# An encoder trunk in fp32: HGRN output as plain products, last value panels as block products, a root on PSUM

## The chip, the cores and the metric

The kernel runs on one core of a Trainium2 chip. The metric is the device time of one execution in microseconds (us). Five engines work side by side: TensorE (PE, matmuls into PSUM banks; PEld is its weight load), VectorE (DVE), ScalarE (ACT), GpSimd (POOL), and SyncE (SP), which issues the DMAs. Each engine executes its own list of instructions in order and waits on semaphores for the others.

## The reference

The trunk has four sub-layers with residuals on a sequence of T = 1024 tokens and D = 1024 channels: a gMLP mixer, a gated ConvFFN, an HGRN2 mixer and a second ConvFFN. Each begins with an RMSNorm whose shift, scale and gate come from a conditioning vector (adaLN, 96 rows of modulation in blocks of 128, each a dot product of a 128x1024 weight block with the vector).

```python
# gMLP:  z = gelu(h @ w_in); u, v = split(z); v = layernorm(v)
s = jnp.einsum('hnm,bcmhd->bcnhd', ws, v) + b_s.T[None, None, :, :, None]
return (u * s.reshape(bsz, t, GM_WIDTH)) @ w_out
# HGRN2: q, fz, i, g = split(h @ w_in, 4); o = gated linear scan over 8 heads
o = o * lax.rsqrt(jnp.mean(o * o, axis=-1, keepdims=True) + EPS)
o = (o.reshape(bsz, t, HG_HEADS * HG_VAL) * gn_g.astype(jnp.float32)).astype(h.dtype)
return (o * jax.nn.silu(g)) @ w_out
# ConvFFN: y = causal conv of width 3 over h @ w_up; (gelu(gate) * val) @ w_down
```

All inputs, parameters and the output are fp32.

## The kernel before

The activations stay in SBUF as `xT`: channels on partitions, 8 tiles of 128 channels, 1024 tokens in two halves of 512 (LO and HI). Matrix products run as three products of split operands, hi·hi, hi·lo and lo·hi (`mm3`, L273). `p_split` makes the parts: ScalarE writes the rounded hi (L471), DVE or GpSimd subtracts it from the source to get lo (L474).

Most products are block products: a pair of 2×2 blocks is multiplied with 7 products instead of 8. That needs sums of operand blocks (`p_comb`, L481, also inside `combos` and `sums`) and additions of results. `Pairs` does it for the up products (`GmUp` for the gMLP, `HgUp` for HGRN, `Ffn`), and `block_out` for the output and down products.

The stages in order, with their places in the profiled execution:

- values, 19 to 252 us: the gMLP's v, 32 tiles of 128 tokens by 512 channels in 4 panels; the first half of the tokens of panels 0 and 1 goes along with the first norm. The rest follows behind the second half's norm. Panels 2 and 3 use plain products (`v_tile`). Beside them DVE works off modulation dots (`ada_dot`, L281), 512 KB loaded for each.
- `GmUp`, 252 to 393: u in 8 pairs, of which the first two are plain (`nplain`), with the spatial product and the gate multiply (L1258). The normalised x is made once more for the block sums: `entry` loads x again and DVE re-normalises it (L1276). Gated blocks and their sums go to DRAM (`gact`).
- `block_out` of the gMLP, 393 to 564, with the next norm (L334 statistics, ten DVE instructions L307 to L317 as inverse root, L339, L344 broadcast, L348 copy) behind its halves; first FFN up (to 985) and down (to 1206).
- HGRN, 1206 to 1683: 16 scan units (8 heads × 2 halves). A unit's output passes a transpose (L1654) and a multiply with the gate (L1656), and goes to DRAM as `hact`, 7 blocks per two heads, sums made on the way.
- HGRN output, to 1833: `block_out` over 4 pairs of heads, each evacuation adding to `xT` on DVE (L413, `p_evac`). Second FFN up and down, final norm.

The order of the instructions of each engine is not written by hand. A `Plan` takes each operation with engine, estimated cost, reads, writes and a priority, schedules the lists against one another twice (the second time by how late an operation may be for PE's list), and emits the lists. A changed cost or priority so moves instructions on all engines.

## Time and profile before

| what | value |
|---|---|
| time, median of 3 runs (lowest to highest) | 2420.84 us (2420.24 to 2420.99) |
| profiled execution, its own time | 2421.06 us |
| its span, first to last instruction | 2419.3 us |
| mean granted TensorE clock | 0.993 |
| DVE, ACT, POOL busy | 2062.3, 1280.9, 458.5 us |
| DMA | 340.34 MB, mean 141 GB/s |

A row of the groups gives line, engine, operation, output<-inputs, tile shape and count, then busy time and mean nanoseconds of one, then the idle time ahead of the group on its engine and who ended it. In a timeline a row is a run of equal instructions with its start, its duration and, in brackets, the wait before it. In the windows an engine's busy time in a stretch stands beside the number of its instructions, then PE's granted clock, the DMA share and the rate.

### The profile page before, as it was taken

The page shows a single profiled execution, that of the slowest core. Times are in us where ns is not written, and L with a number is a line of the kernel's source. Part 1 is how long each engine was busy: PE and PEld are TensorE (multiplying, and loading weights), DVE is VectorE, ACT ScalarE, POOL GpSimd, SP SyncE. Part 2 cuts the span into 40 slices and gives each one's busy share as a digit, 9 for nine tenths or more (in the row PEclk, how much of TensorE's full clock was granted, in tenths as well). Part 3 has the DMA queues.
Part 4 walks back from the last instruction along what each step waited for, and adds up shares of the span by engine and source line. Part 5 has one row for each costly group of instructions (what it writes and reads, how often), then busy time and mean ns, then how long its engine had stood idle before and what let it go on. Part 6 is the DMA issues. An engine that isn't in the chain of part 4 may idle for free.

```text
span 2419.3 us, 32969 instructions
## 1 busy us (share of the span) xinstructions
PE 2381.5 (98%) x11382; PEld 1983.2 (82%) x11382; DVE 2062.3 (85%) x3331; ACT 1280.9 (53%) x2274; POOL 458.5 (19%) x303
## 2 busy tenths in 40 slices
PE   9999999999999999999999999999999999999998
PEld 7888787888888888888788888888777888888887
DVE  8888997898998898976798777879899988989756
ACT  4424664455555455445566666666455554554544
POOL 0122110222222222013201111111322222220121
PEclk9999999999999999999999999999999999999999
DMA  9797678721333333844201111215403333338332
GB/s 354 274 347 274 222 239 299 263 82 35 101 118 114 105 104 116 293 131 140 82 19 49 57 47 54 70 58 182 132 18 105 113 114 105 105 118 291 96 103 98
DMA packets 160873, 340.34 MB, mean 141 GB/s; under 512 B 16193, under 2 KB 35009, under 8 KB 160706
## 3 DMA queue, kind: packets, MB, share of 16 engines
q1 hardware_dynamic: 160706, 338.25, 42.3%
q8 instruction: 89, 1.46, 0.2%
q14 instruction: 78, 0.64, 0.1%
HBM read 259.01 MB, written 79.17 MB: 140 GB/s over the span
## 4 chain that ended last, share of the span: by engine, by line
PE 89%; DVE 5%; DMA 2%; issue 2%; ACT 1%; POOL 0%; SPq 0%; POOLq 0%; DVEq 0%; ACTq 0%
PE pb L273 82%; PE pb L1546 4%; PE pb L1242 1%; DVE n L474 1%; PE pb L1611 1%; DMA raw<-in_ada 1%; PE pb L1631 1%; DVE raw L876 1%; DVE w L474 1%; DVE h L474 0%; PE pb L1633 0%; DMA h<-act 0%; DVE w L481 0%; DVE h L281 0%; PE pb L1453 0%
## 5 line engine op out<-in xcount | busy, mean ns | idle before, releaser
L273 PE MATMUL pb<-h,w 128*128 128x512 f32 (+1 forms) x4338 | 1011.7, 389 | 5.3 <-ACT h L471 2.9
L273 PEld LDWEIGHTS pb<-h,w 128*128 128x128 f32 x4338 | 809.0, 188 | 177.6 <-ACT h L471 4.2
L273 PE MATMUL pb<-n,w 128*128 128x512 f32 x3312 | 791.7, 392 | 6.6 <-DVE n L474 2.5
L273 PEld LDWEIGHTS pb<-n,w 128*128 128x128 f32 x3312 | 617.2, 188 | 138.5 <-DVE n L474 4.1
L474 POOL TENSOR_TENSOR w<-w,w 128x512 fp32r<-128x512 f32 x158 | 248.6, 1579 | 888.5 <-ACT w L471 771.6
L471 ACT ACTIVATE w<-w 128x512 fp32r<-128x512 f32 x384 | 237.0, 627 | 236.1 <-PE pb L273 135.5
L876 DVE SCALAR_TENSOR_TENSOR raw<-wk,prm,raw 128x1024 f32<-128x1024 f32 x168 | 267.8, 1604 | 6.0 <-ACT raw L872 5.0
L474 DVE TENSOR_TENSOR w<-w,w 128x512 fp32r<-128x512 f32 x226 | 162.9, 726 | 35.8 <-ACT w L471 34.9
L273 PE MATMUL pb<-w,n 128*128 128x512 f32 x768 | 177.8, 393 | 4.2 <-DVE n L459 3.6
L471 ACT ACTIVATE w<-n 128x512 fp32r<-128x512 f32 x136 | 85.9, 631 | 168.8 <-PE pb L273 158.2
L273 PEld LDWEIGHTS pb<-w,n 128*128 128x128 f32 x768 | 145.1, 189 | 36.0 <-DVE n L459 4.0
L711 ACT ACTIVATE wk<-pb 128x512 f32<-128x512 f32 x160 | 94.4, 593 | 134.1 <-PE pb L273 111.8
L474 DVE TENSOR_TENSOR w<-n,w 128x512 fp32r<-128x512 f32 x136 | 99.0, 730 | 65.7 <-ACT w L471 65.1
L714 DVE TENSOR_TENSOR wk<-pb,wk 128x512 f32<-128x512 f32 x160 | 108.3, 686 | 44.9 <-PE pb L273 40.6
L474 POOL TENSOR_TENSOR w<-raw,w 128x512 fp32r<-128x512 f32 (+1 forms) x52 | 84.6, 1636 | 275.6 <-ACT w L471 204.3
L471 ACT ACTIVATE h<-h 128x512 fp32r<-128x512 f32 x198 | 121.7, 617 | 16.1 <-DMA h<-act 5.3
L872 ACT ACTIVATE raw<-wk,prm 128x1024 f32<-128x1024 f32 x84 | 103.6, 1240 | 31.7 <-DVE raw L481 15.1
L474 DVE TENSOR_TENSOR h<-h,h 128x512 fp32r<-128x512 f32 x150 | 108.0, 723 | 4.8 <-ACT h L471 4.8
L474 POOL TENSOR_TENSOR h<-h,h 128x512 fp32r<-128x512 f32 x48 | 69.6, 1449 | 215.8 <-ACT h L471 208.9
L413 DVE SCALAR_TENSOR_TENSOR xT<-pb,mod,xT 128x512 f32<-128x512 f32 (+1 forms) x120 | 83.0, 729 | 25.1 <-PE pb L273 24.7
L281 DVE SCALAR_TENSOR_TENSOR h<-h,raw 128x1024 f32<-128x1024 f32 x81 | 102.6, 1293 | 1.0 <-DMA h<-in_ada 0.9
L1556 ACT ACTIVATE wk<-wk 128x256 f32<-128x256 f32 x192 | 75.1, 417 | 42.9 <-PE pb L1546 33.6
(261 smaller groups left out, 2969.5 us busy)
## 6 DMA issues: line engine op xcount, KB each, us to landing
w<-in_up SPq DMA_DIRECT2D x88, 512.0 KB, 3.7
h<-in_ada SPq DMA_DIRECT2D x81, 512.0 KB, 6.0
act<-raw SPq DMA_DIRECT2D x154, 256.0 KB, 2.2
h<-act SPq DMA_DIRECT2D x124, 256.0 KB, 2.7
n<-in_down SPq DMA_DIRECT2D x64, 256.0 KB, 5.3
h<-gact SPq DMA_DIRECT2D x56, 256.0 KB, 3.5
gact<-xT SPq DMA_DIRECT2D x52, 256.0 KB, 3.7
vd<-h SPq DMA_DIRECT2D x32, 256.0 KB, 4.1
```

The costliest lines, as they stand in the source:

```text
L273: PE.matmul(ps, L[i // 2], R[i % 2], start=first and i == 0 and not more, stop=last and i == 2, skip_group_check=more)
L281: V.scalar_tensor_tensor(out=raw, in0=raw, scalar=1.0, in1=condr, op0=ALU.mult, op1=ALU.mult, accum_out=mod[:, m:m + 1])
L413: V.scalar_tensor_tensor(out=xT[:, d, hs], in0=ps.f, scalar=gate(d), in1=xT[:, d, hs], op0=ALU.mult, op1=ALU.add)
L471: pl.op("S", 0.2 + 0.43 * w, lambda: S.activation(hi.r, src.f, AF.Copy), r=(src,), w=(hi,), pr=pr)
L474: lambda: e.tensor_tensor(out=lo.r, in0=src.f, in1=hi.f, op=ALU.subtract), *preds,
L711: pl.op("S", 0.6, lambda: S.activation(c.f, ps.f, func), r=(ps,), w=(c,), pr=p(i) - 10)
L714: pl.op("V", 0.69, lambda: V.tensor_tensor(out=c.f, in0=ps.f, in1=c.f, op=ALU.add), r=(ps, c), w=(c,), pr=p(i) - 8)
L872: pl.op("S", 1.22, lambda: S.activation(y.f, wk[:, o + PADW:o + PADW + T], AF.Identity, bias=pc("conv_b", l * NUP + b), scale=cw(2)), r=(c ...
L876: pl.op("V", 1.26, lambda w=w: V.scalar_tensor_tensor(out=y.f, in0=wk[:, o + w:o + w + T], scalar=cw(w), in1=y.f, op0=ALU.mult, op1=ALU.ad ...
L1242: PE.matmul(ps.f[:, i * P:(i + 1) * P], v.f[:, i * P:(i + 1) * P], wsT[:, j, :], start=True, stop=True)
L1546: PE.matmul(ps_()[0:m, c, :], K.f[:, c * P:c * P + m], q, start=True, stop=True)
L1556: S.activation(halves_(X2, s)[:, :, i, :], halves_(X, s)[:, :, i, :], AF.Copy)
```

## The change

Five parts.

1. The HGRN output becomes plain: for each head and each block of 128 output channels one `mm3` into a bank that sums over 8 heads. A head's output is stored as it is (two blocks per head, the last two heads stay in SBUF) and split on the way back. Weights come in 8 loads of 512 KB instead of 16 of 256 KB.
2. Value panels 2 and 3 of the values become block products, as do pairs 0 and 1 of `GmUp`; both share the block sums of the normalised x, which stays in `xT` instead of being made again (`entry` is gone).
3. In the values the inverse root of the second half's norm takes its intermediate values from PSUM (`psum_ops`, 13 instructions, cost 2.5 instead of 1.95 in the plan).
4. GpSimd's splits in the values go by 128x512 instead of 128x1024 (`half_split`).
5. The modulation dots are spread: 27 instead of 61 in the values, 7 instead of 6 in `GmUp`, 24 instead of 13 in the gMLP's output product, 22 instead of none in the first down product, for which the conditioning row passes through DRAM (`crow`). The plan counts their loads as 1.5 us later (`ADA_LAG`).

```diff
+ADA_LAG = 1.5
+NV_ADA = (18, 3)
+NU_ADA = 1
+NO_ADA = 24
+VS_ENG = "VVGGG"
...
-        return self.LOAD if eng == "D" else self.LAT if e2 != eng else self.CHAIN if eng == "V" else 0.0
+        return self.LOAD + self.late.get(i, 0) if eng == "D" else self.LAT if e2 != eng else self.CHAIN if eng == "V" else 0.0
...
-    hacts = dram.tile([NH // 2, 7, P, HT], F32, name="hact")
+    crow = dram.tile([1, D], F32, name="cr")
+    hacts = dram.tile([NH - 2, 2, P, HT], F32, name="hact")
...
+    def psum_ops(ps, n, scale):
+        m, r, q, u = (small[:, i * 4:i * 4 + n] for i in range(4))
...
+            lambda: V.tensor_copy(m, mp),
+            lambda: V.tensor_scalar(out=rp.bitcast(I32), in0=mp.bitcast(I32), scalar1=-0.5,
+                                    scalar2=float(0x5F3759DF - 2 ** 30 - 2 ** 22), op0=mul, op1=add),
+            lambda: V.tensor_copy(r, rp),
+            lambda: V.tensor_tensor(out=tp, in0=rp, in1=r, op=mul),
...
-            p_load(pl, x, a["ada"][l, blk], pr)
-            p_dot(m, x, pr + 2)
+            pl.late[p_load(pl, x, a["ada"][l, blk], pr)] = ADA_LAG
+            p_dot(m, x, pr + 2, cond=cond)
...
+        p_stats(pl, nm1, accv, bv(7), rbv[1], VB, inps=True)
...
+        def half_split(x, ws, eng, pr):
+            for o in (0, HT):
+                p_split(pl, sub(x, o, HT), *(sub(w, o, HT) for w in ws), eng, pr)
...
+        for i, (n, bn, g, more) in enumerate((("S2", "T2", 0, True), ("S1", "T1", 1, False), ("S3", "T3", 0, True),
+                                              ("A22", "T4", 0, True), ("S4", "B22", 1, True))):
...
+            for c in range(2):
+                ws = ring.next()
+                half_split(raws[n][c], ws, VS_ENG[i], pr - 4 + 2 * c)
+                for t in range(4):
+                    mms(ws, up.b[bn], c, t, 4 * g + t, c == 0, c == 1, more, pr + 2 * c + 0.5 * t)
...
-            self.acts, self.nplain = (gacts, "gact"), 2
+            self.acts = gacts, "gact"
...
-        def entry(self, k, pr):
...
+    p_ada(Seq(whole(nc_[0], F32), whole(nc_[2], F32)), len(ada_todo), DB, cond=cond)
...
-            if u % 4 == 1:
-                p_comb(pl, gout[0, 0], go, gout[0, 0], ALU.subtract, pr)
-                self.store(m, 3, gout[0, 0], pr)
...
+            if h < NH - 2:
+                pl.op("D", 0.73, lambda: nc.sync.dma_start(hacts[h, hf], go.f), r=(go,), w=(("hact", u, u + 1),), pr=pr)
...
-    block_out(pl, OB, NH // 2, lambda m, k, o: a["ho"][2 * m + k, :, o:o + HT],
...
+    def ho_mm(h, hf, d, first, final, b, pr):
+        (wh, wl), (th, tl) = (wtop if d < 4 else wlow)[h], hact[hf][h]
+        c, ps = slice(d % 4 * P, (d % 4 + 1) * P), bv(b)
+        pl.op("PE", 0.681, lambda: mm3(ps.f, (wh.r[:, c], wl.r[:, c]), (th.r, tl.r), first, final), r=(wh, wl, th, tl),
+              w=(ps,), pr=pr)
...
+    for h in range(NH):
+        for d in range(4):
+            ho_mm(h, 0, d, h == 0, h == NH - 1, 4 + d, OB + h + 0.25 * d)
```

In the changed kernel the line numbers move: `mm3` is at L280, `p_evac` at L442, the sums of squares at L459, the splits at L500 and L503, block sums at L510, the output transpose at L1749 and its multiply at L1751.

First place: DVE's list behind the inverse root of the last scan unit, where the HGRN output runs. Before (n, w and raw are operand buffers, `xT` the residual and the scan's working space):

```order
L317 SCALAR_TENSOR_TENSOR small<-small 128x4
L474 TENSOR_TENSOR n_12588<-n_12835,n_12546 128x512
L474 TENSOR_TENSOR n_12591<-w_12367,n_12455 128x512
L474 TENSOR_TENSOR n_12607<-n_12840,n_12573 128x512
L474 TENSOR_TENSOR n_12664<-w_12367,n_12579 128x512
L481 TENSOR_TENSOR n_12898<-n_12686,n_12669 128x512
L1656 SCALAR_TENSOR_TENSOR xT<-pb_77,prm,w_12418 128x512
L413 SCALAR_TENSOR_TENSOR xT<-pb_76,mod,xT 128x512
L481 TENSOR_TENSOR raw_67<-xT 128x512
L474 TENSOR_TENSOR n_12684<-n_12898,n_12593 128x512
L474 TENSOR_TENSOR n_12699<-w_12378,n_12596 128x512
```

The same place now (h_12906 is the sum of squares of the next norm):

```order
L324 SCALAR_TENSOR_TENSOR small<-small 128x4
L503 TENSOR_TENSOR h_12888<-w_12410,h_12888 128x512
L442 SCALAR_TENSOR_TENSOR xT<-pb_79,mod,xT 128x512
L442 SCALAR_TENSOR_TENSOR xT<-pb_80,mod,xT 128x512
L442 SCALAR_TENSOR_TENSOR xT<-pb_81,mod,xT 128x512
L1751 SCALAR_TENSOR_TENSOR xT<-pb_77,prm,w_12424 128x512
L442 SCALAR_TENSOR_TENSOR xT<-pb_82,mod,xT 128x512
L442 SCALAR_TENSOR_TENSOR xT<-pb_75,mod,xT 128x512
L503 TENSOR_TENSOR w_12925<-xT,w_12925 128x512
L459 TENSOR_TENSOR h_12906<-h_12906,raw_66 128x512
L442 SCALAR_TENSOR_TENSOR xT<-pb_76,mod,xT 128x512
L459 TENSOR_TENSOR h_12906<-h_12906,raw_66 128x512
```

Ahead of the unit's output multiply (L1656, now L1751) stood four splits and a block sum of the output product; now stand a split and evacuations, and behind it one split of the unit's own output. The other splits of the product are ahead of the unit's root, within the scan.

Second place: GpSimd's list in the values, from its first split on. Before:

```order
L474 TENSOR_TENSOR w_205<-raw_65,w_176 128x1024
L474 TENSOR_TENSOR w_200<-raw_66,w_166 128x1024
L474 TENSOR_TENSOR w_232<-raw_65,w_198 128x1024
L474 TENSOR_TENSOR w_275<-raw_66,w_225 128x1024
L474 TENSOR_TENSOR w_317<-raw_65,w_243 128x1024
L474 TENSOR_TENSOR w_357<-raw_66,w_273 128x1024
```

Now:

```order
L503 TENSOR_TENSOR w_622<-raw_66,w_611 128x512 x2
L503 TENSOR_TENSOR w_665<-raw_65,w_651 128x512 x2
L503 TENSOR_TENSOR w_767<-raw_65,w_736 128x512 x2
L503 TENSOR_TENSOR w_791<-raw_66,w_761 128x512 x2
L503 TENSOR_TENSOR w_861<-raw_65,w_837 128x512 x2
L503 TENSOR_TENSOR w_938<-raw_66,w_910 128x512 x2
```

Each row of 128x1024 is two of 128x512 in its place, each with a wait of its own; from the seventh on (not shown) the new rows read block sums (w) and no longer the loaded panel alone.

More of the change, by code (lines that the diff above doesn't have):

```diff
@@ L117, in __init__ @@
         self.ops = []
+        self.late = {}
         self.segs = {}
@@ L596, in block_out, with ln_p @@
         return last(last_mm, lambda: n_op[0])
-    def ln_p(nm, l, sub, rbv, tiles, pr, hl="V"):
-        for d in range(KT):
+    def ln_p(nm, l, sub, rbv, tiles, pr, hl="V", order=range(KT)):
+        for d in order:
             t = tiles(d)
@@ L1182, in __init__ @@
             self.sides()
-            self.u, self.vb, self.t1 = (self.halves(*ks) for ks in ((0, 1, 4, 5), (2, 3), (6, 7)))
-            self.temps = [two(self.bc[9], F32), [rv(0, 0, HT), rv(0, HT, HT)], self.t1[2:4]]
-            self.t, self.gate, self.left = {}, {}, 0
+            self.u, self.vb, t_ = (self.halves(*ks) for ks in ((0, 1, 4, 5), (2, 3), (6, 7)))
+            self.temps = [t_[2:4], t_[0:2]]
+            self.t = {k: ((x0(k, LO), x0(k + 4, LO)), (x0(k, HI), x0(k + 4, HI))) for k in TOP}
+            self.gate, self.left = {}, 0
         def halves(self, *ks):
@@ L1261, in done @@
             if not self.left:
-                self.sums(j, self.places(j), *self.temps[min(j, 2)], pr)
+                self.sums(j, self.places(j), *self.temps[j % 2], pr)
         plainfunc = AF.Gelu
-        def entry(self, k, pr):
-            pl = self.pl
-            tv = [rv(i, o, 512) for i in range(2) for o in (0, 512)] if k != 1 else \
-                self.u[4:8]
-            self.t[k] = (tv[0], tv[1]), (tv[2], tv[3])
-            for hf in range(2):
-                for i in range(2):
-                    v, d, rb = tv[2 * hf + i], k + 4 * i, rbv[hf]
-                    p_load(pl, v, a["x"][:, d, halves[hf]], pr - 6)
-                    pl.op("V", 0.69, lambda v=v, d=d, rb=rb: V.scalar_tensor_tensor(
-                        out=v.f, in0=v.f, scalar=amul[:, d:d + 1], in1=rb.f, op0=ALU.mult, op1=ALU.mult),
-                        r=(v, rb), w=(v,), pr=pr, port=True)
-            self.combos(k, pr, self.t1[k])
@@ L1311, in trunk @@
     up = GmUp(pl, UB)
-    up.start()
+    values()
     up.up()
@@ new lines, in trunk, with ho_act @@
+    braw = Seq(*two(fr[11], F32))
+    def ho_act(h, hf, pr):
+        x, eng = gout.get((h, hf)), "V"
+        if h < NH - 2:
+            x = braw.next()
+            p_load(pl, x, hacts[h, hf], pr - 3, r=(("hact", 2 * h + hf, 2 * h + hf + 1),))
+            eng = "VG"[hf and h % 2]
+        p_split(pl, x, *hact[hf][h], eng, pr)
+    def ho_mm(h, hf, d, first, final, b, pr):
[3 more added lines that the diff above has]
+              w=(ps,), pr=pr)
@@ new lines, in ho_out @@
+    def ho_out(d, hf, b, pr):
+        p_evac(pl, bv(b), d, halves[hf], gate1(1), (1, 2), pr)
+    for m in range(NH):
+        ho_weights(m, OB - 16 + m)
+        ho_act(m, 0, OB - 16 + m)
+    ho_act(NH - 2, 1, OB - 8)
+    for d in range(KT):
+        p_load(pl, xv(d, LO), xspill[:, d, LO], OB - 11, r=(("xs", 2 * d, 2 * d + 1),))
+    for h in range(NH):
+        for d in range(4):
+            ho_mm(h, 0, d, h == 0, h == NH - 1, 4 + d, OB + h + 0.25 * d)
+    for d in range(4):
+        ho_out(d, 0, 4 + d, OB + 4)
@@ new lines, in trunk @@
+    for d in range(4, KT):
+        for h in range(NH):
+            ho_mm(h, 0, d, h == 0, h == NH - 1, d - 4, OB + 2 * d)
+        ho_out(d, 0, d - 4, OB + 2 * d - 2)
+    for h in (0, 1, 2, 3, 4, 5, 7):
+        ho_act(h, 1, OB + 8 + h)
+    for d in range(KT):
+        p_load(pl, xv(d, HI), xspill[:, d, HI], OB + 4, r=(("xs", 2 * d + 1, 2 * d + 2),))
+    for h in range(NH):
+        for d in range(4, KT):
+            ho_mm(h, 1, d, h == 0, h == NH - 1, d, OB + 16 + h + 0.25 * (d - 4))
+    for d in range(4, KT):
+        ho_out(d, 1, d, OB + 20)
@@ L1724, in trunk, with ho_tail @@
+    ho_first(OB + 12)
+    for h in range(NH - 2):
+        for d in range(4):
+            ho_mm(h, 1, d, h == 0, False, d, OB + 24 + h + 0.25 * d)
+    n_op = [OB + 30]
+    def ho_tail(d):
+        for h in range(NH - 2, NH):
+            n_op[0] += 0.25
+            ho_mm(h, 1, d, False, h == NH - 1, d, n_op[0])
+        return bv(d)
+    ho_last(ho_tail, lambda: n_op[0])
     f1.pads()
```

280 lines of the change are left out of this document (168 added, 112 removed).

## The prediction

> **What bounds the kernel now.** I read first the page's busy times and its chain of waits, then the windows by stage, then TensorE's timeline wherever a window held more time than its matmuls need.
>
> ```profile
> PE 2381.5 (98%) x11382; PEld 1983.2 (82%) x11382; DVE 2062.3 (85%) x3331; ACT 1280.9 (53%) x2274; POOL 458.5 (19%) x303
> PE 89%; DVE 5%; DMA 2%; issue 2%; ACT 1%; POOL 0%; SPq 0%; POOLq 0%; DVEq 0%; ACTq 0%
> ```
>
> TensorE (PE) sets the end. A matmul fewer is worth its pitch, and a microsecond in which PE waits is worth a microsecond; work of the other engines counts only where it makes PE wait. The pitch comes from an undisturbed stretch of PE's timeline (start, duration, operation, count):
>
> ```profile
> 1824.73 5.60 PE L273 MATMUL pb<-n,w 128*128 128x512 f32 x24
> 1830.17 2.88 PE L273 MATMUL pb<-h,w 128*128 128x512 f32 x12
> ```
>
> 24 starts in 1830.17 − 1824.73 = 5.44 us make 0.227 us per 128x512 matmul (the 390 ns of the page's groups are overlapping durations, so no price). Where does PE take longer than this? The windows (span, then PE, PEld, DVE, ACT, POOL busy, granted clock, DMA share, GB/s) and PE's groups in the first of them:
>
> ```profile
> 1687.00:1833.00 146.00, 133.69 (x564) 106.13 (x563) 134.09 (x194) 74.99 (x123) 38.10 (x21) 0.96 0.24 78
> 1702.00:1744.00 42.00, 40.67 (x170) 33.21 (x171) 34.85 (x56) 18.43 (x32) 10.77 (x8) 0.92 0.36 114
> 1810.00:1834.00 24.00, 20.11 (x78) 14.85 (x76) 23.05 (x30) 12.31 (x19) 3.14 (x2) 0.93 0.19 62
> ```
>
> ```profile
> L273 PE MATMUL pb<-n,w 128*128 128x512 f32 x252 | 59.9, 395 | 2.8 <-DVE n L474 2.3 <-DVE n L459 0.5
> L273 PE MATMUL pb<-n,n 128*128 128x512 f32 x240 | 59.8, 408 | 8.8 <-DVE n L474 6.3 <-ACT n L471 2.5
> L273 PE MATMUL pb<-h,w 128*128 128x512 f32 x48 | 12.9, 417 | 0.6 <-DVE h L474 0.6
> L344 PE MATMUL pb<-h,ones 128*128 128x512 f32 x4 | 2.1, 618 | 0.1
> ```
>
> This is the HGRN output and the start of the second FFN: 540 matmuls at 0.227 make 122.6 us of the 146. The four broadcasts (L344) are 2.1 us busy and some 20 narrow ones less, so **19 to 23 us** go in waits and slow clock; I take 21. Stalls alone (last bracket: idle before, and what ended it):
>
> ```profile
> 1690.25 0.74 PE L273 MATMUL pb<-n,n 128*128 128x512 f32 x2 [3.05 <-DVE n L474]
> 1701.48 0.51 PE L273 MATMUL pb<-n,n 128*128 128x512 f32 x1 [2.54 <-ACT n L471]
> 1703.22 2.08 PE L273 MATMUL pb<-n,n 128*128 128x512 f32 x4 [1.24 <-DVE n L474]
> 1747.11 1.16 PE L273 MATMUL pb<-n,n 128*128 128x512 f32 x3 [1.98 <-DVE n L474]
> 1816.84 0.96 PE L273 MATMUL pb<-n,w 128*128 128x512 f32 x3 [1.40 <-DVE n L474]
> 1818.70 1.22 PE L273 MATMUL pb<-n,w 128*128 128x512 f32 x2 [0.91 <-DVE n L474]
> ```
>
> They sum to 11.1 us. The clock adds (1 − 0.92) × 42 = 3.4 and (1 − 0.93) × 24 = 1.7: after the stall at 1701 four matmuls take 2.08 us where 0.9 is the pitch. Each stall is ended by a split (L471, L474), DVE being 92% busy here (134.09 of 146).
>
> **The HGRN output.** It was 4 pairs × 7 products × 4 blocks × 3 = 336 matmuls and becomes 8 heads × 8 blocks × 2 halves × 3 = 384: +48 × 0.227 = **+10.9 us** on the bound. What it removes is DVE work. Between the last scan unit's root and the root of the second half's norm, DVE's list holds 110 instructions before and 59 now: 32 splits (L474) become 2, 15 block sums (L481) become 2, 21 evacuations (L413) become 16. From DVE's groups in the window 1687 to 1833:
>
> ```profile
> L474 DVE TENSOR_TENSOR n<-w,n 128x512 fp32r<-128x512 f32 x20 | 20.4, 1034 | 0.6 <-ACT n L471 0.6
> L413 DVE SCALAR_TENSOR_TENSOR xT<-pb,mod,xT 128x512 f32<-128x512 f32 x21 | 14.9, 743 | 4.7 <-PE pb L273 4.6
> L474 DVE TENSOR_TENSOR n<-n,n 128x512 fp32r<-128x512 f32 x12 | 10.9, 921 | 1.5 <-ACT n L471 1.5
> L481 DVE TENSOR_TENSOR w<-w,n 128x512 f32<-128x512 f32 x4 | 2.7, 678 | 0.0
> ```
>
> That is 30 × 0.98 + 13 × 0.68 + 5 × 0.74 = 42 us less DVE work in a stretch where DVE ended PE's waits. The remaining splits stand earlier, in the scan, whose window shows DVE at 83% (394.69 of 477):
>
> ```profile
> 1206.00:1683.00 477.00, 475.57 (x2853) 411.62 (x2852) 394.69 (x952) 301.25 (x671) 58.97 (x43) 1.00 0.20 65
> ```
>
> The 82 us that DVE has free there cover what moves in. What stays are two places without cover. First, the last scan unit: its output transpose (L1749 now) stands behind 24 plain matmuls, 5.4 us, after the unit's last product, while what has to come between follows one after another. Before, it was this (DVE, then ScalarE, ACT):
>
> ```profile
> 1684.30 0.68 DVE L1637 TENSOR_REDUCE small<-h 128x4 f32<-128x512 f32 x1
> 1687.83 0.69 DVE L474 TENSOR_TENSOR n<-n,n 128x512 fp32r<-128x512 f32 x1
> ```
>
> ```profile
> 1687.95 1.14 ACT L1648 ACTIVATE xT<-pb,small 128x128 f32<-128x128 f32 x4
> ```
>
> From the reduction to the first row behind the root's ten instructions pass 3.5 us, to the end of the scaling 4.8; with the copy ahead of the reduction (0.6) and two splits now queued there (2 × 0.68) it is 6.8, so a wait of 1 to 3 us. Second, the handover to the FFN. The same handover after the first block output had one stall:
>
> ```profile
> 624.48 3.71 PE L273 MATMUL pb<-n,w 128*128 128x512 f32 x15 [1.03 <-ACT wk L711]
> 396.43 0.50 PE L273 MATMUL pb<-h,w 128*128 128x512 f32 x1 [2.51 <-ACT h L471]
> ```
>
> I take 2 us for it, and 1 for clock. So 21 becomes 5: **−16 us**. The bounds: −21 if nothing waits, 0 if the waits come from latency and not from load. I choose near the first, since five of the six stalls were ended by a DVE split that queued behind other DVE work.
>
> **The values and the gMLP's up product.** The last value panels as block products take 48 matmuls less and the first two pairs 24 less: −72 × 0.227 = **−16.3 us**. With the 48 added, PE executes 24 fewer: 24 × 0.227 = **5.4 us** net. But do DVE and GpSimd keep up with the shorter PE time?
>
> ```profile
> 0.00:252.00 252.00, 245.96 (x1107) 203.92 (x1108) 214.31 (x382) 103.80 (x169) 45.17 (x26) 0.98 0.88 310
> 252.00:393.00 141.00, 139.79 (x712) 116.69 (x711) 131.99 (x208) 85.38 (x179) 23.22 (x18) 1.00 0.73 238
> ```
>
> ```profile
> L281 DVE SCALAR_TENSOR_TENSOR h<-h,raw 128x1024 f32<-128x1024 f32 x71 | 88.2, 1271 | 0.1
> L474 DVE TENSOR_TENSOR w<-h,w 128x1024 fp32r<-128x1024 f32 x10 | 11.9, 1217 | 0.0
> L1276 DVE SCALAR_TENSOR_TENSOR raw<-raw,amul,h 128x512 f32<-128x512 f32 x9 | 6.6, 744 | 2.5 <-DMA raw<-in_x 2.5
> ```
>
> Up to the last gate multiply DVE's list loses 29 modulation dots (L281) and 16 re-normalisations (L1276), and gains 43 two-operand 128x512 and 8 128x1024 instructions: −29 × 1.27 − 16 × 0.74 + 43 × 0.68 (the L481 row above) + 8 × 1.22 = −10 us. So 346 of 393 us (88%) becomes 336 of 377 (89%): it fits, with 41 us free instead of 47. The load is more uneven, however: from the second half's root to the first gate multiply the same prices give DVE 133 us (105 before) while PE's own work there falls from 127 to 113. DVE's operands for the first block product of panels 2 and 3 (S2) stand 45 to 47 us behind the root where PE arrives at 56, later ones lead by 6 to 9 us; evacuations fall behind, and eight banks absorb part. I charge **+2 us**, bounds −1 (PE's idle time in the second window, 141 − 139.8) and +20 (133 − 113).
>
> The 12 GpSimd splits of 128x1024 become 24 of 128x512. Beside a GpSimd instruction, DVE rows with two operands in SBUF swell:
>
> ```profile
> 157.10 0.16 DVE L289 TENSOR_TENSOR mod<-mod,prm 128x8 f32<-128x8 f32 x1
> 157.29 2.36 DVE L293 SCALAR_TENSOR_TENSOR amul<-mod,prm 128x8 f32<-128x8 f32 x1
> ```
>
> ```profile
> 157.23 4.76 POOL L474 TENSOR_TENSOR w<-raw,w 128x1024 fp32r<-128x1024 f32 x2 [27.27 <-ACT w L471]
> ```
>
> ```profile
> L474 POOL TENSOR_TENSOR w<-raw,w 128x512 fp32r<-128x512 f32 x40 | 53.4, 1344 | 123.4 <-ACT w L471 123.2 <-DVE small L308 0.2
> L474 POOL TENSOR_TENSOR w<-raw,w 128x1024 fp32r<-128x1024 f32 x12 | 31.1, 2612 | 152.2 <-ACT w L471 81.2 <-DVE wk L430 71.0
> ```
>
> A DVE row of 0.2 us lasts 2.36, as long as the GpSimd row beside it. 24 × 1.34 = 32.3 us against 31.1: the sum of such blocking hardly changes, one block lasts half as long, and the first halves are ready sooner. Nothing for the sum. The Trainium skill, "SBUF — State Buffer", section "Who interferes with whom", says that a DVE instruction with two SBUF inputs contends with a GpSimd one that reads SBUF, and one with at most one SBUF input does not; the 2.36 us row agrees. By that rule the root on PSUM operands is also safe from a block.
>
> The second half's root becomes 13 instructions on PSUM instead of ten. Three more of the size of the 0.16 us row make +0.5 us; ten more at a full evacuation's 0.74 would be the far end, +7. I take the near one, since the operands have four columns. Between the statistics and the broadcast PE has 30 matmuls, 6.8 us, of cover; without it the 0.5 would show, and a block of 2.2 us (2.36 − 0.16) that it avoids would be its gain. Zero.
>
> **The modulation dots** that leave the values go to the first block output (13 to 24) and the first down product (0 to 22), each with a 512 KB load on SP's queue and 1.27 us of DVE.
>
> ```profile
> 1078.00:1109.00 31.00, 31.00 (x139) 25.67 (x138) 16.43 (x23) 15.26 (x27) 11.48 (x9) 1.00 0.41 122
> 1109.00:1140.00 31.00, 31.00 (x143) 25.79 (x142) 16.04 (x29) 15.54 (x27) 9.41 (x6) 1.00 0.51 150
> ```
>
> Here 22 × 1.27 = 28 us meet 29.5 us of free DVE (62 − 32.5) and a DMA share near one half. The first block output's window is
>
> ```profile
> 393.00:564.00 171.00, 168.27 (x737) 137.98 (x737) 145.23 (x228) 81.11 (x140) 35.76 (x25) 0.99 0.57 189
> ```
>
> so 11 × 1.27 = 14 us meet 26 free; its opening wait, 396.43 above, stays. Zero for both; without cover up to 5 us, inside the +20.
>
> **Sum:** 2421.06 (the profiled execution, span 2419.3) − 5.4 − 16 + 2 = 2401.7; less 0.2, since the median shown is 2420.84: **2401.5 us**.
>
> **Rivals.**
>
> *DVE limits values and up product a little.* For it: 133 against 113 us. Against it: the lead of 6 to 9 us of the operands. PE then waits for half of the 20 instead of the 2 charged: 2409.5.
>
> *The HGRN waits are latency.* A scan tail and a norm end there as before; against it speak the five splits queued on DVE. The 21 us stay: 2421 − 5.4 = 2415.6.
>
> *Slower: DVE becomes the bound from the second half's root on.* Its place is the first gate multiply, its price the full 20 us, plus the blocks of the twelve GpSimd halves that stand in this stretch, at most 12 × 1.34 = 16 us, of which I take half, since a DVE row is hit only where both meet. It decides once DVE's lag exceeds the 6 to 9 us by which the operands lead. Then 2401.5 − 2 + 20 + 8 = 2427.5. The Trainium skill's rule on two SBUF inputs speaks for it: all added sums have two. Against it: the whole stage still has 41 us free.
>
> *Better than forecast:* all of the 21 go, and the 2.5 us before 396.43 too, with nothing charged: 2421 − 5.4 − 21 − 2.5 = 2392.
>
> **How the numbers follow.** Forecast 0.56, DVE a little late 0.18, latency 0.12, DVE bound 0.08, better 0.06. Some 0.2% (4.8 us, so 2416.0 and 2425.7) is what a measurement can tell from no change. The latency case lies on the bound, half on each side: faster 0.56 + 0.18 + 0.06 + 0.06 = 0.86, same 0.06, slower 0.08. The range goes from the better case's 2392 to 2416, which leaves out the slower case and parts of both ends; the forecast's own range is 2396 to 2406.
>
> **What would show it.** Right: 4398 matmuls pb<-h,w, some 5 us of excess from the scan's end to the FFN's first pairs, DVE clearly below 90% there, and a norm root at the values without a stall. Wrong: PE idle ended by DVE evacuations or L503 between the second half's root and the last gate multiply (DVE bound), idle at L1749 or the FFN's first products of more than 10 us (latency), half-clock rows behind either, or loads for dots that delay weights in the first down product.

## The result, and the profile after

The changed kernel takes 2408.14 us (median of four executions, 2403.49 to 2410.95) against 2420.91 of the kernel before: ratio 0.9945, 95% interval 0.9932 to 0.9957, about 13 us faster. The forecast was 2401.5 in a range of 2392 to 2416, so the direction and the range held and the gain came out at two thirds of the forecast. The profiled execution is the one of 2403.49 us (span 2401.4), the shortest of the four, so the traces below show less loss than the median has; a second trace, at 2408.04 us, follows with the first experiment. One execution of the run with four dots per pair took 4489.35 us at a granted clock of 0.837 and is left out of that run's figures.

The page and the chain of waits look as before, with TensorE still setting the end:

```profile
PE 2370.1 (99%) x11358; PEld 1977.2 (82%) x11358; DVE 2048.6 (85%) x3300; ACT 1287.2 (54%) x2293; POOL 455.0 (19%) x312
PE 87%; DVE 6%; DMA 3%; issue 2%; ACT 1%; SPq 0%; POOL 0%; POOLq 0%; DVEq 0%; ACTq 0%
```

PE's groups by shape show the matmuls that the change moved (h,w 4266 to 4398, w,n 768 to 612, n,n 336 to 96; with w,h 336 to 480, w,w 42 to 78 and 60 new h,n, not shown, the sum is 24 fewer):

```profile
L280 PE MATMUL pb<-h,w 128*128 128x512 f32 x4398 | 1030.3, 391 | 5.7 <-ACT h L500 2.2 <-DVE w L503 1.3 <-ACT wk L740 0.8
L280 PE MATMUL pb<-w,n 128*128 128x512 f32 x612 | 142.9, 394 | 4.2 <-DVE n L488 3.6 <-ACT xT L1173 0.5
L280 PE MATMUL pb<-n,n 128*128 128x512 f32 x96 | 25.1, 402 | 0.0
```

Now the two stages on which the sum rested. Windows of the changed kernel (columns as before): the scan, the HGRN output with the FFN's first pairs, the middle of the values, and the end of the first down product.

```profile
1206.00:1668.00 462.00, 462.00 (x2778) 400.56 (x2778) 376.81 (x925) 299.64 (x665) 61.67 (x44) 1.00 0.18 57
1668.00:1815.00 147.00, 146.41 (x670) 120.86 (x668) 103.57 (x164) 65.22 (x107) 28.06 (x20) 1.00 0.19 56
100.00:200.00 100.00, 94.37 (x393) 74.59 (x392) 92.85 (x144) 43.57 (x80) 29.66 (x20) 0.97 0.70 230
1110.00:1215.00 105.00, 102.01 (x454) 83.03 (x453) 97.61 (x150) 60.32 (x106) 29.54 (x20) 1.00 0.41 132
```

```profile
1753.95 1.13 PE L373 MATMUL pb<-h,ones 128*128 128x512 f32 x2 [0.59 <-DVE h L368]
```

In the HGRN output DVE is 70% busy (103.57 of 147) where it was 92%, the granted clock is 1.00 where it was 0.96, and the wait of 0.59 us is the only one that PE's timeline marks between 1668 and 1800. The values turned the other way. The same 100 us of the kernel before, and PE's four longest sums of waits in the whole changed kernel, of which only the first lies between 100 and 200 us:

```profile
100.00:200.00 100.00, 100.00 (x443) 82.84 (x442) 80.53 (x136) 30.43 (x46) 32.28 (x14) 1.00 0.88 303
```

```profile
PE pb L1148 <- DVE wk L1145: 4.5, 1, 4.5
PE pb L373 <- DVE h L368: 3.9, 3, 2.5
PE pb L280 <- DVE n L488: 3.6, 1, 3.6
PE pb L280 <- ACT h L500: 2.2, 2, 1.4
```

393 matmuls instead of 443 start in the same 100 us, so some 50 × 0.227 = 11 us are lost there, and DVE went from 81% to 93%. The waits of 3.6 and 2.5 us, for L488 and L368, stand at 25 and 2392 us, and the kernel before has both at the same length.

To compare stages of different kernels I worked out from each trace the time from each matmul's start to the next one's, less the pitch of its shape (0.227 us for 128x512), and summed it by stage. All times in us; "before" and "changed" are their profiled executions (2421.06 and 2403.49), the others are runs that follow.

| stage (window of the changed kernel) | before | HGRN output alone | changed | no late dots | three dots per pair |
|---|---|---|---|---|---|
| start and first values, 0 to 100 | 14.7 | 16.1 | 12.1 | 15.0 | 13.6 |
| values, 100 to 200 | −0.1 | −0.1 | 11.2 | 0.7 | 0.7 |
| up product and its end, 200 to 430 | 8.8 | 5.9 | 3.6 | 8.7 | 3.4 |
| output product, first FFN up, 430 to 1100 | 3.4 | 4.0 | 4.9 | 5.2 | 13.4 |
| end of first FFN down, 1100 to 1230 | 2.6 | 2.7 | 4.8 | 14.8 | 4.6 |
| scan, 1230 to 1668 | 8.4 | 8.6 | 8.8 | 10.7 | 9.0 |
| HGRN output, 1668 to 1850 | 22.2 | 2.2 | 2.0 | 2.6 | 1.8 |
| rest | 4.1 | 3.9 | 4.5 | 4.0 | 3.9 |
| all | 64.1 | 43.4 | 51.7 | 61.8 | 50.6 |

Check: 24 matmuls less (5.4) and 64.1 − 51.7 = 12.4 less lost make 17.8; the profiled executions differ by 17.6.

### The profile page after: what moved, and what is told of

Its sections match the earlier page's. It is cut to its first block, busy times and chain, and to the rows that moved or that the text cites. A ratio compares the mean times of both kernels' runs of the same rounds, so it can differ in the third digit from the quotient of the medians.

```text
span 2401.4 us, 32825 instructions
## 1 busy us (share of the span) xinstructions
PE 2370.1 (99%) x11358; PEld 1977.2 (82%) x11358; DVE 2048.6 (85%) x3300; ACT 1287.2 (54%) x2293; POOL 455.0 (19%) x312
## 4 chain that ended last, share of the span: by engine, by line
PE 87%; DVE 6%; DMA 3%; issue 2%; ACT 1%; SPq 0%; POOL 0%; POOLq 0%; DVEq 0%; ACTq 0%
PE pb L280 79%; PE pb L1641 4%; DVE h L503 1%; PE pb L1359 1%; DVE w L503 1%; DMA n<-in_wo 1%; DMA gact<-xT 1%; PE pb L1726 1%; PE pb L1706 1%; PE pb L1728 1%; DVE wk L288 0%; DMA h<-act 0%; DVE xT L478 0%; DMA xT<-vd 0%; DVE h L288 0%
## 5 line engine op out<-in xcount | busy, mean ns | idle before, releaser
L280 PE MATMUL pb<-h,w 128*128 128x512 f32 (+1 forms) x4470 | 1039.4, 389 | 5.7 <-ACT h L500 2.2
L280 PEld LDWEIGHTS pb<-h,w 128*128 128x128 f32 x4470 | 832.3, 188 | 181.3 <-ACT h L500 3.5
L280 PE MATMUL pb<-n,w 128*128 128x512 f32 x3312 | 790.2, 392 | 2.0 <-ACT wk L740 1.0
L280 PEld LDWEIGHTS pb<-n,w 128*128 128x128 f32 x3312 | 617.9, 188 | 131.1 <-ACT wk L740 1.4
L503 POOL TENSOR_TENSOR w<-w,w 128x512 fp32r<-128x512 f32 x170 | 262.8, 1551 | 951.5 <-ACT w L500 826.1
L500 ACT ACTIVATE w<-w 128x512 fp32r<-128x512 f32 x405 | 249.6, 627 | 262.5 <-PE pb L280 167.8
L503 DVE TENSOR_TENSOR w<-w,w 128x512 fp32r<-128x512 f32 x235 | 168.3, 723 | 35.4 <-ACT w L500 34.4
L500 ACT ACTIVATE w<-n 128x512 fp32r<-128x512 f32 x136 | 85.9, 632 | 170.8 <-PE pb L280 152.7
L280 PE MATMUL pb<-w,n 128*128 128x512 f32 x612 | 142.9, 394 | 4.2 <-DVE n L488 3.6
L280 PEld LDWEIGHTS pb<-w,n 128*128 128x128 f32 x612 | 115.5, 189 | 31.0 <-DVE n L488 4.0
L503 DVE TENSOR_TENSOR w<-n,w 128x512 fp32r<-128x512 f32 x136 | 98.5, 727 | 44.1 <-ACT w L500 43.8
L500 ACT ACTIVATE h<-h 128x512 fp32r<-128x512 f32 x198 | 122.1, 617 | 17.4 <-DMA h<-gact 5.7
L503 POOL TENSOR_TENSOR w<-raw,w 128x512 fp32r<-128x512 f32 x55 | 79.1, 1449 | 233.2 <-ACT w L500 150.6
L280 PE MATMUL pb<-w,h 128*128 128x512 f32 x480 | 118.4, 398 | 0.7 <-DVE w L503 0.5
L503 DVE TENSOR_TENSOR h<-h,h 128x512 fp32r<-128x512 f32 x150 | 108.2, 724 | 3.3 <-ACT h L500 3.2
L442 DVE SCALAR_TENSOR_TENSOR xT<-pb,mod,xT 128x512 f32<-128x512 f32 (+1 forms) x108 | 74.5, 727 | 40.1 <-PE pb L280 39.9
L503 POOL TENSOR_TENSOR h<-h,h 128x512 fp32r<-128x512 f32 x48 | 68.8, 1434 | 205.9 <-ACT h L500 194.7
L280 PEld LDWEIGHTS pb<-w,h 128*128 128x128 f32 x480 | 87.9, 188 | 19.9 <-DVE w L503 1.3
```

The lines of the kernel that those rows point to most:

```text
L280: PE.matmul(ps, L[i // 2], R[i % 2], start=first and i == 0 and not more, stop=last and i == 2, skip_group_check=more)
L442: V.scalar_tensor_tensor(out=xT[:, d, hs], in0=ps.f, scalar=gate(d), in1=xT[:, d, hs], op0=ALU.mult, op1=ALU.add)
L500: pl.op("S", 0.2 + 0.43 * w, lambda: S.activation(hi.r, src.f, AF.Copy), r=(src,), w=(hi,), pr=pr)
L503: lambda: e.tensor_tensor(out=lo.r, in0=src.f, in1=hi.f, op=ALU.subtract), *preds,
```

## The experiments

**The changed kernel once more**, unaltered, to see whether its spread has one place.

> The changed kernel once more, unaltered, since its four executions spread over 2403.5 to 2411.0 us while those of the kernel before spread over 2.6. Theory: the spread comes from one place, the values, where TensorE waits 4.5 us for the memset of the spatial weights (L1148 behind L1145) and where VectorE and GpSimd meet; a new trace of a slower execution then shows 3 to 7 us more waits and half-clock matmuls between 80 and 200 us, and the rest of the kernel equal within 1 us. Rival: the whole kernel is slower or faster, and the extra time lies in many places. Time 2403 to 2411.

2410.95 us (2408.04 to 2416.51, five executions), ratio to the kernel before 0.9956 [0.9944, 0.9969]. Its profiled execution took 2408.04, 4.6 more than the first profile. The lost time is 56.4 instead of 51.7, but not at one place: 13.4 instead of 12.1 up to 100 us, 9.4 instead of 11.2 in the values, 6.7 instead of 3.6 to 430, 5.4 instead of 4.9 to 1100, 5.5 instead of 4.8 to 1230, 2.7 instead of 2.0 in the HGRN output. The wait at L1148 is the same:

```profile
154.97 3.59 PE L1148 MATMUL pb<-wk,ones 128*128 128x512 f32 x4 [4.47 <-DVE wk L1145]
```

The theory that this wait makes the spread fell here; the rival, many places, is what the two traces show. Two of the places go with the granted clock: behind the same wait it stays at one half for 6.8 us in the first trace (0.86 over 150 to 175) and for 3.4 us in the second (0.93), and ahead of 390 only the second has it below 1 (0.91 over 380 to 400), 1.7 us each way. The kernel before spreads too, if less: beside this run over 2418.41 to 2423.96. What makes an execution of 2416 stays open.

**The plain HGRN output alone**, put into the kernel before.

```diff
-    hacts = dram.tile([NH // 2, 7, P, HT], F32, name="hact")
+    hacts = dram.tile([NH - 2, 2, P, HT], F32, name="hact")
...
-    block_out(pl, OB, NH // 2, lambda m, k, o: a["ho"][2 * m + k, :, o:o + HT],
...
+    for h in range(NH):
+        for d in range(4):
+            ho_mm(h, 0, d, h == 0, h == NH - 1, 4 + d, OB + h + 0.25 * d)
```

> The kernel before with the plain HGRN output alone (48 matmuls more than before, no block sums). Theory: +10.9 us of matmuls and about -20 us of waits, so 2411 to 2413, with less than 3 us of TensorE excess between the last scan unit and the first FFN pairs. Rival: those waits came from latency and were not removed by this part but by something else in the changed kernel: 2425 to 2432.

2412.61 us (2411.60 to 2413.62), ratio 0.9961 [0.9947, 0.9974], against 2422.42 in the same comparison: −9.8. By parts: +10.9 for the matmuls, 22.2 to 2.2 in the output, −20.0. Its window of the output:

```profile
1685.00:1830.00 145.00, 144.54 (x647) 118.91 (x646) 102.36 (x159) 64.25 (x103) 29.25 (x21) 1.00 0.17 53
```

So the waits went with DVE's work and were not latency. It also says what the other parts were worth: in the same comparison the whole changed kernel took 2410.95, 1.7 us less than this one, with 72 matmuls (16.3 us) fewer. By the medians almost all of these 16.3 us were lost elsewhere; the two traces of the changed kernel, both of shorter executions than its median, have 8.3 and 13.0 us more lost time than this one (51.7 and 56.4 against 43.4).

**The second half's root in SBUF again.**

```diff
-        p_stats(pl, nm1, accv, bv(7), rbv[1], VB, inps=True)
+        p_stats(pl, nm1, accv, bv(7), rbv[1], VB)
```

> The changed kernel with the second half's root of the values in SBUF again (10 instructions instead of 13). Theory: no difference (2408, within 3), since TensorE has 30 matmuls of cover there. Rival: the root is held up by GpSimd's splits, 1.3 us at each meeting; TensorE then waits at the broadcast L373, and the time is 2 to 6 us longer.

2409.28 us (2406.97 to 2413.66), ratio 0.9949 [0.9935, 0.9963], beside 0.9956 for the changed kernel in the same comparison: no difference. Both halves of the expectation's question have an answer in the traces. Root rows in the changed kernel (first, fifth and last of 13) with a row in SBUF soon after, GpSimd's splits at the same time, and three of the root's ten rows in this kernel:

```profile
79.34 0.17 DVE L333 TENSOR_SCALAR pb<-pb 128x4 f32<-128x4 f32 x1 [1.45 <-PE pb L363]
...
80.02 0.17 DVE L338 TENSOR_TENSOR pb<-pb,small 128x4 f32<-128x4 f32 x1
...
81.63 0.16 DVE L346 SCALAR_TENSOR_TENSOR small<-pb,small 128x4 f32<-128x4 f32 x1
...
81.94 1.11 DVE L1137 TENSOR_TENSOR lbt<-lbt 128x8 f32<-128x8 f32 x1
```

```profile
77.91 5.11 POOL L503 TENSOR_TENSOR w<-raw,w 128x512 fp32r<-128x512 f32 x4 [77.47 <-DVE wk L288]
```

```profile
80.89 0.91 DVE L315 TENSOR_SCALAR small<-small 128x4 int32<-128x4 int32 x1
81.84 1.30 DVE L317 TENSOR_TENSOR small<-small 128x4 f32<-128x4 f32 x1
83.18 1.22 DVE L318 TENSOR_TENSOR small<-small 128x4 f32<-128x4 f32 x1
```

The root on PSUM takes 2.45 us (79.34 to 81.79), undisturbed though GpSimd works from 77.91 to 83.02; the two-operand row in SBUF at 81.94 takes 1.11. The root in SBUF takes 4.9 (80.70 to 85.58) with ten instructions, since three of them are held up beside the same splits. It is blocked, as the rival said, but the 30 matmuls cover it, and PE marks no wait at the broadcast L373. By the Trainium skill, "SBUF — State Buffer", section "Who interferes with whom", DVE instructions with two SBUF inputs contend with a GpSimd instruction that reads SBUF, and those with at most one only in a mode with two ports, which a tensor_scalar can enter; the trace has L317 and L318 at 1.30 and 1.22 and the single-input L315 at 0.91, and none of the thirteen on PSUM above 0.17. The prediction left that exception out; whether L315 ran in such a mode no trace shows.

**The spatial weights' matmuls one product later.** In the changed kernel, PE's 4.5 us at L1148 are a wait for a memset (L1145) of the spatial weights, whose row sums these matmuls make:

```profile
148.93 1.76 DVE L503 TENSOR_TENSOR h<-xT,h 128x512 fp32r<-128x512 f32 x1
150.61 2.28 DVE L288 SCALAR_TENSOR_TENSOR wk<-wk,raw 128x1024 f32<-128x1024 f32 x1
152.82 0.08 DVE L288 DVE_READ_ACCUMULATOR wk<-wk,raw 128x1 f32 x1
152.82 0.68 DVE L503 TENSOR_TENSOR h<-xT,h 128x512 fp32r<-128x512 f32 x1
153.67 0.48 DVE L1145 MEMSET wk<- 64x512 f32 x1 [0.16 <-DVE h L503]
```

```profile
148.54 3.27 POOL L503 TENSOR_TENSOR w<-w,w 128x512 fp32r<-128x512 f32 x2 [30.91 <-ACT w L500]
```

```profile
134.04 11.16 SPq L514 DMA_DIRECT2D wk<-in_ada  x4
146.02 0.33 SPq L1144 DMA_DIRECT2D wk<-in_wsT  x1
```

The memset stands behind two splits and a dot in DVE's list; the first split and the dot are longer by 1.1 us each beside two GpSimd halves; and the load of the weights was issued only behind four loads for dots, which take up 11 us of SyncE's list. The load did not hold the memset in this execution, though: DVE passed its wait for it at 151.06, and had no idle time of more than 0.2 us between 140 and 153.7.

```diff
-            if i == 1:
-                mixer((4, 5), b0 + 2)
+            if i == 2:
+                mixer((4, 5), b0 + 4)
```

This kernel leaves one thing out: the row sums overwrite two banks in which partial sums of a value panel stand, so a part of that panel's products is lost, with every instruction in place.

> The changed kernel with the spatial weights' preparation (load, memset, row sums) planned one product later, so that its two matmuls L1148 stand 30 matmuls (6.8 us) later in TensorE's list. Theory: the wait of 4.5 us and the half clock behind it vanish, -5 to -8 us: 2400 to 2403, with a spread under 3 us. Rival: VectorE's lag there is carried to the next product and TensorE waits there instead: 2407 to 2409, spread unchanged.

2401.39 us (2400.26 to 2403.12), ratio 0.9916 [0.9902, 0.9929]; −9.6 against the changed kernel beside it, with a spread of 2.9 us; time and spread are those of the theory. The lost time between 100 and 200 us is 2.9, and PE marks no wait at L1148:

```profile
155.38 2.02 PE L1148 MATMUL pb<-wk,ones 128*128 128x512 f32 x4
```

The memset itself came no earlier (153.31, where it was 153.67); only the matmuls that need it stand later. The profiled executions (2408.04 and 2401.39) differ by 6.6 of the 9.6 us, with 6.5 less lost in this stage; against the first trace (2403.49) it is 2.1, with 8.3 less lost here and 4.2 more up to 430.

**Load and memset earlier**, the version without anything left out.

```diff
-        pl.op("D", 1.46, lambda: nc.sync.dma_start(wsT, a["wsT"]), w=(wsv,), pr=pr)
-        pl.op("V", 0.4, lambda: V.memset(wsT[64:128, :, 0:64], 0.0), w=(wsv,), pr=pr)
...
                 p_ada(Seq(*abufs), 6, VB + 14)
+                mixer_load(VB + 14)
```

> The changed kernel with the load and the memset of the spatial weights planned behind the first six modulation dots, so that VectorE has the memset 36 instructions earlier and SyncE the load ten issues earlier; the scheduler then puts the two matmuls L1148 ahead of the first block product of panels 2 and 3. Nothing is left out. Theory: the memset stood behind modulation dots and splits in VectorE's list and its load behind four loads of dots in SyncE's list; without that the wait of 4.5 us and the half clock behind it are gone: 2400 to 2403, spread under 4 us. Rival: the wait reflects VectorE's lag as a whole, and TensorE now waits as long at the next product's operands: 2407 to 2411.

2408.56 us (2405.24 to 2415.15), ratio 0.9954 [0.9941, 0.9966]: no gain over the changed kernel. The wait at L1148 is gone, but PE waits shortly afterwards, in the first block product of panels 2 and 3:

```profile
145.25 4.81 PE L280 MATMUL pb<-w,h 128*128 128x512 f32 x20 [0.47 <-DVE w L503]
150.80 0.49 PE L280 MATMUL pb<-w,h 128*128 128x512 f32 x1 [0.73 <-ACT w L500]
152.53 0.88 PE L280 MATMUL pb<-w,h 128*128 128x512 f32 x2 [1.24 <-POOL w L503]
```

5.9 us are lost between 100 and 200 instead of 9.4 to 11.2, with the granted clock at 0.50 from 153 to 156 again, and more is lost at other places (7.3 at the end of the first down product; whether the one follows from the other is not shown). The rival holds in part: about half of the loss stayed, with waits ended by splits, as a DVE that is late as a whole would have it. But the run before this one speaks against it: with the matmuls later in the list the wait did not move on. The two runs differ in more than this place, since the plan orders all lists anew, and why one kept its gain is open.

**No modulation dots beside the last block products.**

```diff
-NV_ADA = (18, 3)
+NV_ADA = (18, 0)
```

> The changed kernel with 18 modulation dots in the values instead of 27 (none beside the last block products); the nine run in the first down product. Theory: a dot of 2.3 us and its load stand right ahead of the memset, so its wait shrinks by 2 to 4 us: 2402 to 2406. If the lag of VectorE is general, the gain is larger than the wait (9 x 1.2 = 11 us of its work): 2398 to 2402. If dots are covered everywhere: 2408 to 2411.

2412.23 us (2409.05 to 2414.05), ratio 0.9964 [0.9951, 0.9977]. No faster than the changed kernel, where 2398 to 2406 was expected, yet with the values as expected:

```profile
100.00:200.00 100.00, 100.00 (x443) 82.22 (x443) 89.35 (x141) 49.92 (x90) 31.84 (x22) 1.00 0.69 213
1110.00:1215.00 105.00, 97.47 (x407) 77.72 (x406) 93.93 (x143) 54.07 (x91) 33.64 (x20) 0.95 0.46 144
```

Nine dots less, 11 us of DVE, took the whole loss of these 100 us away (11.2 to 0.7): the dots were the cause, and since the weights' load was in time in the changed kernel, more likely by their work on DVE than by their loads. The nine dots were planned into the first down product, where the loss rose from 4.8 to 14.8, half of it by the granted clock (0.05 × 105 = 5.3 us). Between 200 and 430 this trace loses 8.7 us, where the two of the changed kernel lose 3.6 and 6.7.

```profile
1188.75 7.10 PE L280 MATMUL pb<-n,w 128*128 128x512 f32 x23 [3.00 <-DVE n L488]
1197.18 1.05 PE L363 MATMUL pb<-ones,h 128*128 128x1 f32 x8 [1.33 <-DVE h L459]
1205.88 0.50 PE L280 MATMUL pb<-n,w 128*128 128x512 f32 x1 [2.30 <-ACT h L1578]
```

```profile
1202.90 1.23 DVE L288 SCALAR_TENSOR_TENSOR h<-h,h 128x1024 f32<-128x1024 f32 x1 [1.38 <-DMA h<-in_ada]
```

In this last row a dot holds DVE for its load (1.38 us) while the next norm's operands stand behind it.

**Whole GpSimd splits.**

```diff
         def half_split(x, ws, eng, pr):
+            if eng == "G":
+                p_split(pl, x, *ws, eng, pr)
+                return
```

> The changed kernel with GpSimd's splits of the values in whole 128x1024 instructions again (12 instead of 24; VectorE's own splits stay halved). Theory: the sum of what GpSimd blocks is the same, so the difference is small, 0 to +4 us (2408 to 2413). Rival: the longer block delays VectorE where it has no lead: 2414 to 2422.

2406.53 us (2404.66 to 2406.68), ratio 0.9940 [0.9927, 0.9953]: within the changed kernel's first interval and just below the second. The groups of GpSimd between 60 and 200 us, changed and whole:

```profile
L503 POOL TENSOR_TENSOR w<-raw,w 128x512 fp32r<-128x512 f32 x15 | 21.7, 1465 | 100.4 <-DVE wk L288 77.5 <-ACT w L500 22.9
L503 POOL TENSOR_TENSOR w<-w,w 128x512 fp32r<-128x512 f32 x12 | 18.5, 1564 | 52.4 <-ACT w L500 40.8 <-DVE xT L676 11.6
```

```profile
L503 POOL TENSOR_TENSOR w<-raw,w 128x1024 fp32r<-128x1024 f32 (+1 forms) x9 | 20.7, 2303 | 102.2 <-ACT w L500 102.1
L503 POOL TENSOR_TENSOR w<-w,w 128x1024 fp32r<-128x1024 f32 x6 | 16.2, 2708 | 52.8 <-ACT w L500 45.0 <-DVE xT L676 7.8
```

The sums are 40.2 and 36.9 us. Halving the splits brought nothing that can be measured. This plan, too, has no wait for the memset (L1148 waits 0.3 us, for ACT), and yet loses 8.6 us between 100 and 200, with PE's waits ended by splits (L500, L503) and ScalarE's rows L1173: a second sign that the wait at the memset is not the whole of the lag.

**The dots back in the values.**

```diff
-NV_ADA = (18, 3)
+NV_ADA = (40, 3)
```

> The changed kernel with 49 modulation dots in the values instead of 27 and none in the first down product. Theory: VectorE has no room for 22 x 1.2 = 26 us more while TensorE's part of the values is 16 us shorter than before: 2420 to 2435, with waits on its splits and evacuations between 100 and 380 us, and nothing gained in the down product. Rival: the values still have the slack that its 85% mean share suggests: 2406 to 2412.

2464.08 us (2457.91 to 2465.33), ratio 1.0171 [1.0157, 1.0186], far more than the 2420 to 2435 of the theory. 22 dots make some 26 us of DVE work; the lost time rose by 60 (111.5 against 51.7), of which 40.5 are lost between 100 and 200 us, where it was 11.2. The longest wait runs over the end of these 100 us:

```profile
210.31 4.98 PE L280 MATMUL pb<-w,n 128*128 128x512 f32 x14 [17.64 <-DVE wk L1150]
```

There DVE's list has the copies of the row sums (L1150) behind a row of dots, and one of the dots waits for its load:

```profile
206.88 1.23 DVE L288 SCALAR_TENSOR_TENSOR wk<-wk,raw 128x1024 f32<-128x1024 f32 x1 [3.56 <-DMA wk<-in_ada]
```

The spread of the dots is thus the part that makes the shorter values possible at all. The end of the first down product, without dots, loses 0.3 us instead of 4.8, where the theory expected no gain.

**Two and three dots per pair in the up product**, and the first of them with whole GpSimd splits.

```diff
-NV_ADA = (18, 3)
-NU_ADA = 1
+NV_ADA = (18, 0)
+NU_ADA = 2
```

> The changed kernel with 18 modulation dots in the values instead of 27 and two per pair in the gMLP's up product (14 instead of 7); the first down product gets 24 instead of 22. Theory: VectorE's room decides stage by stage. TensorE's excess over its pitch between 100 and 200 us falls from 9 to 11 us to about 1 (as with no dots beside the last block products), the up product has 20 us of VectorE free for 7 x 1.2 us more, and the down product gets two dots more, +1 to +2: 2400 to 2404. Rival: any VectorE work in the up product shows there as it did in the down product: 2407 to 2412.

> As the run with two dots per pair in the up product, with three per pair: 21 there, 17 in the first down product instead of 24. Theory: the down product's excess falls from about 5 to about 3 us, and the up product, with 17 us more VectorE work than the changed kernel in 20 us free, starts to wait: 2399 to 2405. Rival: the up product becomes VectorE's bound: 2408 to 2415.

> The run with two dots per pair in the up product and GpSimd's splits in whole 128x1024 instructions. Theory: as without dots beside the last products VectorE has room, the form of GpSimd's splits does not matter: within 2 us of the run with halved splits. Rival: the halved splits pay once VectorE's other load is gone, or cost by their number: more than 3 us to one side.

Two per pair: 2406.26 us (2405.21 to 2407.60), ratio 0.9941 [0.9924, 0.9958], between the expected 2400 to 2404 and the rival's 2407. Between 100 and 200 us 0.7 are lost as expected, the down product 6.9, the output product and first FFN 11.5 instead of 4.9. With whole splits 2406.79, ratio 0.9944 [0.9929, 0.9958]: the same, so the form of the splits does not matter there either. Three per pair: **2399.97 us** (2399.51 to 2402.11), ratio 0.9918 [0.9903, 0.9932], the best kernel of this study that computes everything: 20.7 us below the kernel before beside it, and its interval lies below that of the repeated changed kernel and touches that of the first comparison (0.9932). Its trace, of an execution of 2402.11, loses 50.6 us in all where those of the changed kernel lose 51.7 and 56.4. Its windows:

```profile
100.00:200.00 100.00, 100.00 (x443) 82.27 (x442) 88.93 (x143) 49.98 (x91) 31.76 (x22) 1.00 0.70 217
250.00:380.00 130.00, 128.51 (x641) 107.41 (x640) 116.36 (x187) 76.74 (x160) 21.66 (x15) 1.00 0.82 270
```

The up product took dots without loss: DVE 90% busy, and 1.2 us lost between 200 and 372. But it took fewer than planned: 25 dots start between 200 and 380 where the changed kernel has 18, and 22 between 380 and 560 where it has 17, so that more of the dots now run in the gMLP's output product. From 430 to 1100 13.4 us are lost instead of 4.9, 5.1 of them around a wait in the output product, for an evacuation behind a dot:

```profile
445.50 4.82 PE L280 MATMUL pb<-h,w 128*128 128x512 f32 x13 [3.21 <-DVE xT L442]
```

**Four dots per pair, 18 in the output product.** The aim was that last wait.

```diff
-NU_ADA = 1
-NO_ADA = 24
+NU_ADA = 4
+NO_ADA = 18
```

> As the run with three modulation dots per pair in the up product, with four per pair (28 there), 18 in the gMLP's output product instead of 24 and 16 in the first down product instead of 17. Theory: the output product, where a dot stood ahead of the evacuation that TensorE waited 3.2 us for, falls back from 12 us of excess to about 4, the up product has little room left and gains 1 to 4 us of excess: 2393 to 2400. Rival: the up product becomes VectorE's bound with 34 us more of its work than in the changed kernel's 20 us of room: 2402 to 2412.

2403.51 us (median of five executions, 2401.82 to 2411.39), ratio 0.9930 [0.9915, 0.9945]: above the expected 2393 to 2400 and not to be told apart from three per pair. (21 dots more are 25 us, not the 34 of the expectation.) The up product still loses little (0.9 between 200 and 372), but the wait in the output product stayed:

```profile
444.93 7.29 PE L280 MATMUL pb<-h,w 128*128 128x512 f32 x24 [3.60 <-DVE xT L442]
```

The aim was missed because the dots did not move: 26 start between 200 and 380 and again 22 between 380 and 560, though six fewer are planned into the output product. By these counts some 25 dots find room up to 380, however many are planned.

## Why the prediction was right or wrong

**The count** (−5.4): right; the matmuls are those listed, and the profiled executions add up with it.

**The HGRN output** (21 to 5, −16): right in mechanism, undersized. It measured 22.2 to 2.0, and −20.0 for this part alone. The two places without cover, 1 to 3 us at the last output transpose and 2 at the handover, cost 0 and 0.6: at the transpose PE marks no wait. The forecast had 6.8 us of chain behind 5.4 us of matmuls, with two splits in the chain; they ran ahead of the reduction instead, while DVE waited for the copy. Reduction to end of root took 3.7 us, and the transposes began 5.7 us after the start of the unit's last matmul, right behind the 24 matmuls. The clock, charged with 1 us, stayed at 1.00. The rival that the waits are latency is refuted by the run of this part alone.

**The values and the up product** (+2): much too small, and the working behind it fails. The first trace loses 26.9 us up to 430 instead of 23.4, so +3.5; the second, at 2408.04 us, loses 29.5, so +6.1. Against the medians the terms other than −5.4 and −20.2 sum to 2408.14 − (2420.91 − 25.6) = +12.8 instead of +2. The second trace accounts for most of that: 6.1 here and 4.9 in the two stages that took dots (2.0 from 430 to 1100, 2.9 to 1230).

The forecast compared 336 us of DVE work with 377 and then trusted the lead of 6 to 9 us that DVE's operands have by undisturbed prices. From the second half's root to the first gate multiply it priced 133 us of DVE; the window 79.30 to 234.80 has 141.7. Rows beside GpSimd are longer (the splits h<-xT average 0.95 us between 60 and 200, not 0.68), which the forecast describes and then leaves out of this sum. It also looked for the lag at the wrong place. The first gate multiply came 31 us behind its spatial product (204.0 and 234.8), and PE marks no wait between 200 and 300; PE met the lag at 154 us, at the memset of the spatial weights, which the forecast does not name and which stands behind dots. The mean share of a stage hid this: 89% over 377 us, but 93% of the 100 us in which the block products of panels 2 and 3 run. The rival "DVE limits values and up product a little", 2409.5 us with a chance of 0.18, has the right kind of cause and almost the measured time; but its 10 us lie in these two stages alone, where the traces have 3.5 and 6.1.

That the forecast missed by only 6.6 us is in part luck: the HGRN output gave 4 us more than forecast, and the rest cost some 11 us more.

**The modulation dots** (zero): wrong at the far end. The first down product lost 4.8 instead of 2.6, and nine more dots cost 10 us there. The forecast found 29.5 us free between 1078 and 1140 for 28 us of dots; six of the 22 ran there, twelve ahead of 1078 and four behind 1140. The windows of the end of this product show DVE at 97.61 of 105 us against 78.05 in the kernel with the HGRN output alone:

```profile
1110.00:1215.00 105.00, 103.54 (x461) 84.84 (x460) 78.05 (x130) 59.58 (x102) 24.83 (x17) 1.00 0.32 99
```

Why they ran there is not settled by a run; the dots share two buffers, whose loads stand on SyncE's list, and the late ones meet the next norm.

**The GpSimd splits** (zero): right; whole ones are as fast. **The root on PSUM** (zero for the time, 2.4 us for 13 instructions): right, 2.45, and the block that it avoids is real, 3 us, under cover. **The slower rival** (2427.5) did not come, but the run with the dots back shows that DVE's lag can cost more than the work that was added, 60 us for 26. Not all of it lies where the rival had it: one dot waits 3.56 us for its load, and the start (0 to 100 us) loses some 11 us more. **The opening wait** of the output product (2.5 us at 396.43, "stays") became 1.4 us, ahead of 385.12 in the first trace.
